# A two-layer decoder trunk on one core: late key splits, gate rows 8 to 15 first, paired gate chunks, products that rotate over eight PSUM banks

## The chip, the cores and the metric

The kernel runs on one core of a Trainium2 chip (trn2). The metric is the device time of one execution in microseconds (us); for the kernel before there are three runs, 1920.1, 1920.73 and 1922.91 us, with the median 1920.73 us. One further execution was taken with the hardware profiler; every row quoted below comes from it.

## What is computed

512 tokens of width 2048 go through two layers. Layer 0 mixes by sparse attention (an indexer chooses 128 keys for each query), layer 1 by stick-breaking attention over one shared K and V. Each layer ends in a LayerNorm over the residual and a sigmoid-gated embedding:

```python
for i in range(DEPTH):                      # two layers
    if i < N_A_LAYERS:
        h = mixer_a(x, w_in_a[i], w_o_a[i], positions)
    else:
        if i == N_A_LAYERS:
            k_sh, v_sh = shared_kv(x, w_kv_b)
        h = mixer_b(x, w_in_b[j], w_o_b[j], k_sh, v_sh)   # sigmoid(z) * prod(1 - sigmoid(z)), o * silu(gate)
    x = layer_norm(ALPHA * x + h, ln_g[i], ln_b[i])
    x = x + (p[i] @ w_p) * sigmoid(x @ w_ple_gate[i])
```

Inputs, weights and the output are f32.

## The kernel before, in words

**Layout.** Activations lie transposed: 16 blocks of 128 features by 512 tokens. Each matrix operand is split into a high part and a low part (`split`, line 129: ScalarE copies the high part, VectorE subtracts it from the source), and each product is three matmuls (`mm3`, line 133): high by high, low by high, high by low. `XH[k]` and `XL[k]` are the two parts of block k of the moving operand; `F` holds 16 f32 blocks. Because all splits go through `split`, most ScalarE and VectorE rows of the profile carry line 111, the recording helper; the tile names tell them apart.

**Weights.** Sync's queue loads them in the order of the list `units` (line 161) into three `raw` buffers of 512 KB (`next_raw`, line 178). A transfer is issued when its buffer is free, and behind every transfer listed earlier. `plain_items` splits each row block into `wh` and `wl`, three buffers of each, so the split of one block waits until TensorE is through with the block three before it. `gemm_w` (line 262) walks 16 row blocks; for each, four banks of PSUM take three matmuls of 512 columns each: 12 matmuls for a block.

**Order.** TensorE's order is written out by hand: generators yield after each three matmuls, and `steps`, `interleave` and `pumped` mix them. The other engines' orders come from a scheduler, except for operations recorded while `pinned` is set (`paced`, and what is popped from the queue `bg` by `pumped`); those keep the written order.

**The phases that the change touches**, in order of time:

- *Start* (lines 138 to 148, 554 to 561). A tile `ones` is made, 24 matmuls of 128 columns run on it, then the indexer's first chunk begins while x and its weights still arrive. Rope tables (`rope_tables`, tiles `ang` and `kk`) are computed on VectorE in between.
- *End of a layer* (`finish_layer`, line 747, once for each layer). Output projection, LayerNorm sums by matmuls with `ones`, embedding, and then the gate's chunks. In lines 914 to 922 `normalise(k+1)` (two VectorE operations on a block, two ScalarE operations with the affine, one VectorE subtraction) is recorded ahead of the four steps that use block k, all 16 blocks in the first 512 columns of the gate. The other chunks (512, 512, 256, 256, or 128 twice in layer 1) follow, with `gated` emptying the banks of the chunk before. Weights come in the list's order, chunk after chunk.
- *K, V and the queries* (lines 995 to 1028). K's projection uses banks 4 to 7. V and four query chunks are computed by a Strassen scheme: `gemm_s` (line 344) accumulates seven products `m0` to `m6` for each chunk, in banks 0 to 6 each time (`product_banks`, line 341). `combine` (line 367) empties them: ScalarE copies m0, m3 and m4, VectorE adds m1, m2, m5 and m6 onto those copies. `turn_values` transposes V through bank 7 while the second chunk runs.
- *Ahead of the attention* (lines 1022 to 1062). The Strassen scheme had overwritten columns 256 to 511 of blocks 0 to 7 with sums, so two transfers from `x2` in DRAM bring them back, and eight `split`s put them in place while the last query chunk runs. Then K of all four groups, V and the first queries are split: K of group 0 by `split`, K of groups 1 to 3 by VectorE copies and GpSimd subtractions. `neg` and `tri` (the constant triangles) are made here.
- *Attention of layer 1* (`sticks`, line 1074, four groups). For each of ten units `logits` makes z by three matmuls, and ScalarE's Abs, Exp, Ln, VectorE's max-and-add, on diagonal units GpSimd's triangle, and a `split` make the parts (`sh`, `sl`) that `weights` multiplies onto z; then Exp, a split (`ah`, `al`), and `values`. It is interleaved with a gate chunk of `w_in_b` (line 1143): 20 steps of it (5 row blocks) ahead of group 0, 8 steps ahead of each other group. At a group's end four Silus empty banks 0 to 3.

Of the kernel before, what the change touches and what calls it, by code (L numbers as in the profile page):

```python
# [18 lines left out]
T = 512  # L19
H = T // 2  # L20
# [57 lines left out]
def trunk_kernel(  # L78
# [63 lines left out]
    ones = top.tile([128, 128], F32R, name="ones")  # L142
    onef = top.tile([128, 128], F32, name="onef")
    dve.memset(onef, 1.0)
    dve.tensor_copy(ones, onef)
    spun = bank(7, "spun")
    for _ in range(24):
        pe.matmul(spun[:, :128], ones, ones, start=True, stop=True)
# [5 lines left out]
    def fblock(n):  # L154
        return F[n // 4][:, n % 4]

# [184 lines left out]
    def product_banks():  # L341
        return [bank(i, f"m{i}").rearrange("p (j t) -> p j t", j=2) for i in range(7)]
# [109 lines left out]
    def add_parts(src, parts):  # L452
        for i, n in enumerate(parts):
            add_job(src, sum(parts[:i]), n)

    def add_finish(layer, w_o):
        add_parts(w_o, PARTS)
        add_job(pT[layer], 0, nk=2)
        for c in range(4):
            add_job(w_ple[layer], c * 512, nk=2)  # L460
        add_parts(w_ple_gate[layer], LAST_PARTS if layer else PARTS)
# [92 lines left out]
    bg.append(lambda: None)  # L554
# [192 lines left out]
    def finish_layer(layer, resid, last, keep, early, ahead):  # L747
# [3 lines left out]
        E8 = keep.enter_context(tc.tile_pool(name=f"e8{layer}", bufs=1, side="right")).tile([128, 8, T], F32, name="E8")  # L751
        fp_ = ExitStack()
        fp = fp_.enter_context(tc.tile_pool(name=f"fp{layer}", bufs=1, side="right"))
        E = [E8[:, n] for n in range(8)] + [fp.tile([128, T], F32, name=f"e{n}") for n in range(8, NK)]
# [11 lines left out]
        def total(parts, b, between):  # L766

            h, l = parts
            ps = bank(b, "sum")
            pe.matmul(ps, ones, h, start=True, stop=False)  # L770
            steps(between, 1)
            pe.matmul(ps, ones, l, start=False, stop=True)
            return ps
# [58 lines left out]
        for c, where in ((1, (0, 1, 2, 3)), (2, (4, 5, 6, 7))):  # L832
            banks, gemm = gemm_part(wo, c, 512, where, 3)
            if c == 1:
                steps(gemm, 36)
                ps = total(parts_of(S), 7, gemm)
                act.activation(cen, ps, AF.Copy, scale=1.0 / 512.0)
# [49 lines left out]
        dve.scalar_tensor_tensor(dm, yps, 1.0 / D, cen, ALU.mult, ALU.subtract)  # L887
        dve.tensor_tensor(va, dm, dm, ALU.mult)
        dve.scalar_tensor_tensor(va, qps, 1.0 / D, va, ALU.mult, ALU.subtract)
# [38 lines left out]
        with tc.tile_pool(name=f"pe{layer}", bufs=1, side="right") as ep:  # L928
# [17 lines left out]
            plan = list(zip(parts[1:], ((2, 3, 4, 5), (6, 7, 0, 1), (2, 3), (0, 1)))) + [(0, ())]  # L946
            if layer:
                plan[3:] = [(128, (0,)), (128, (1,)), (0, ())]
            for c, (n, where) in enumerate(plan):
# [12 lines left out]
                banks = [bank(b, "g") for b in where]  # L962
                gemm = pumped(gemm_w(gitems, plain, banks, n), 4 if n == 512 else 2)
# [13 lines left out]
    def first_sums(E8):  # L977
        shared.append(E8)
        C3.extend(c3_tiles(ps_.enter_context(tc.tile_pool(name="sp0", bufs=1)), range(4)))
        flat = E8.rearrange("p n t -> p (n t)")  # L980
        TF.extend(flat[:, n : n + 3 * H].rearrange("p (i t) -> p i t", i=3) for n in (0, 2 * T))
        T1.extend(flat[:, 4 * T + n * H : 4 * T + (n + 1) * H] for n in range(8))
# [8 lines left out]
    pk_ = ExitStack()  # L991
    finish_layer(0, xT, x2, pk_, first_sums, first_blocks)


    with ps_:
        sp = ps_.enter_context(tc.tile_pool(name="sp1", bufs=1))
        C3.extend(c3_tiles(sp, range(4, 8)))
        Kf, Vf = shared[0][:, 0:4], shared[0][:, 4:8]
        banks = [bank(b, "k") for b in (4, 5, 6, 7)]
# [5 lines left out]
        def turn_values(t):  # L1005
            s = slice(t * 128, (t + 1) * 128)
            ps = bank(7, "vt")
# [4 lines left out]
        for n, dst in enumerate((Vf, *F)):  # L1012
            M = product_banks()
# [18 lines left out]
    tri = pc.tile([128, 128], F32R, name="tri")  # L1032
    neg = pc.tile([128, 128], F32R, name="neg")
    trf = pc.tile([128, 128], F32, name="trf")
    pool.memset(trf, -1.0)
    dve.tensor_copy(neg, trf)
    pool.affine_select(out=trf, in_=trf, pattern=[[-1, 128]], compare_op=ALU.is_ge, fill=0.0, base=0, channel_multiplier=1)
    dve.tensor_copy(tri, trf)

    K = [tuple(pc.tile([128, T], F32R, name=f"k{s}{g}") for s in "hl") for g in range(4)]  # L1040
    V = [tuple(pc.tile([128, 4, 128], F32R, name=f"v{s}{t}") for s in "hl") for t in range(4)]
    items = plain_stream(*[(512, NK, False)] * 4)
    split(*K[0], Kf[:, 0])
    for t in range(4):
        split(*V[t], Vf[:, :, t * 128 : (t + 1) * 128])
    def split_dve(hi, lo, src, eng=dve):
        dve.tensor_copy(hi, src)
        eng.tensor_tensor(lo, src, hi.bitcast(F32), ALU.subtract)

    def split_scaled(g):  # L1050
        Q = []
        for i in range(4):
            qh, ql = (pc.tile([128, 4, 128], F32R, name=f"q{s}", tag=f"q{s}", bufs=4) for s in "hl")
            src = F[g][:, :, i * 128 : (i + 1) * 128]
            act.activation(qh, src, AF.Copy, scale=HSCALE)
            dve.scalar_tensor_tensor(ql, src, HSCALE, qh.bitcast(F32), ALU.mult, ALU.subtract)
            Q.append(tuple(a.rearrange("p h q -> p (h q)") for a in (qh, ql)))
        return Q

    Q = split_scaled(0)  # L1060
    for g in range(1, 4):
        split_dve(*K[g], Kf[:, g], pool)
    pk_.close()
    px_ = ExitStack()
    px = px_.enter_context(tc.tile_pool(name="px", bufs=1, side="right"))
# [74 lines left out]
    for g in range(4):  # L1140
        tc.keep_in_program_order(act.preload_act_table_set("natural_log_exp_and_others"))
        banks = mm_banks("g")
        interleave(sticks(g, Q), 30 + 4, gemm_w(items, plain, banks), 52 - 12 * (g == 0), lead=8 + 12 * (g == 0))
        if g < 3:
            Q = split_scaled(g + 1)
# [4 lines left out]
    px_.close()  # L1150
    pc_.close()

    with ExitStack() as keep:
        finish_layer(1, x2, outT, keep, lambda E8: [], lambda gemm: None)
# [46 lines left out]
```

## Time and profile before

| | us |
|---|---|
| median of three runs | 1920.73 |
| the profiled execution, device time | 1921.26 |
| its span (first to last instruction) | 1919.2 |
| TensorE busy | 1903.6 |
| VectorE busy | 1225.6 |
| ScalarE busy | 929.6 |
| GpSimd busy | 34.2 |

2.06 us of the execution lie outside the span. The mean granted TensorE clock is 0.999. Engines in the rows: PE is TensorE, PEld its weight load, DVE VectorE, ACT ScalarE, POOL GpSimd, SP Sync, whose rows with a q are the issues of transfers. A row of the timeline has the start, the duration, engine, line, operation, tiles written and read, shape and count, and in brackets the idle time of the engine before it and what ended that. A row of the windows has, for each stretch, its length, then busy time and number of instructions of PE, PEld, DVE, ACT and POOL, the granted clock, the share of the DMA engines and GB/s. Successive matmuls overlap, so the distance of their starts, and not the duration of one, tells the rate.

### The profile page before, as it was taken

What the parts mean: (1) busy time and instruction counts of PE and PEld (TensorE: products, weight loads), DVE (VectorE), ACT (ScalarE), POOL (GpSimd) and SP (SyncE); (2) the same over time, 40 slices, a digit from 0 to 9 for tenths busy, and PEclk for the clock granted to TensorE, in tenths of its full rate; (3) what the DMA queues carried; (4) which work ended last, traced back from release to release, by engine and by line L of the source; (5) the groups of instructions that cost most, each with busy time, mean ns of one, the idle gap of its engine ahead of it and who ended that gap; (6) DMA issues with size and microseconds to landing.
All of it is one profiled execution on the core that took longest, in us unless ns stands there. A gap on an engine that the chain in (4) does not pass through costs nothing.

```text
span 1919.2 us, 25113 instructions
## 1 busy us (share of the span) xinstructions
PE 1903.6 (99%) x9247; PEld 1594.0 (83%) x9247; DVE 1225.6 (64%) x2385; ACT 929.6 (48%) x1689; POOL 34.2 (2%) x52
## 2 busy tenths in 40 slices
PE   9999999999999999999999999999999999999998
PEld 7788888888888888878888999987888888887887
DVE  6677667985566445576368788876656645568434
ACT  4355222355555433375235444458877743347323
POOL 0000000000000000000000000011100000000000
PEclk9999999999999999999999999999999999999999
DMA  6332333322222342333334333331222153242333
GB/s 195 99 88 67 99 99 99 95 71 66 66 66 67 125 139 88 99 110 121 115 111 126 104 96 100 108 112 47 70 71 63 59 177 98 77 127 93 120 100 110
DMA packets 110587, 189.22 MB, mean 99 GB/s; under 512 B 8240, under 2 KB 28208, under 8 KB 110464
## 3 DMA queue, kind: packets, MB, share of 16 engines
q1 hardware_dynamic: 110320, 187.33, 32.0%
q8 instruction: 72, 1.18, 0.3%
q14 instruction: 51, 0.42, 0.1%
q0 software_dynamic: 144, 0.30, 0.1%
HBM read 179.21 MB, written 8.39 MB: 98 GB/s over the span
## 4 chain that ended last, share of the span: by engine, by line
PE 93%; DVE 3%; DMA 1%; ACT 1%; issue 1%; POOL 0%; SPq 0%; DVEq 0%
PE g L135 12%; PE g L134 12%; PE g L136 12%; PE o L135 7%; PE o L134 7%; PE o L136 7%; PE m L134 3%; PE m L135 3%; PE m L136 3%; PE q L136 3%; PE q L135 3%; PE q L134 3%; PE z L1114 1%; PE k L134 1%; PE k L136 1%; PE k L135 1%
## 5 line engine op out<-in xcount | busy, mean ns | idle before, releaser
L111 ACT ACTIVATE wh<-raw 128x512 fp32r<-128x512 f32 (+2 forms) x684 | 396.4, 581 | 684.7 <-PE g L135 242.6
L111 DVE TENSOR_TENSOR wl<-raw,wh 128x512 fp32r<-128x512 f32 (+2 forms) x684 | 430.2, 630 | 463.6 <-ACT wh L111 448.0
L134 PE MATMUL g<-xh,wh 128*128 128x512 f32 x1024 | 404.9, 395 | 0.3 <-ACT u L111 0.3
L135 PE MATMUL g<-xl,wh 128*128 128x512 f32 x1024 | 402.0, 393 | 2.0 <-DVE xl L111 2.0
L136 PE MATMUL g<-xh,wl 128*128 128x512 f32 x1024 | 400.7, 391 | 1.3 <-DVE wl L111 1.3
L135 PEld LDWEIGHTS g<-xl,wh 128*128 128x128 f32 x1024 | 192.7, 188 | 44.8 <-DVE xl L111 6.9
L136 PEld LDWEIGHTS g<-xh,wl 128*128 128x128 f32 x1024 | 192.5, 188 | 42.2 <-DVE wl L111 1.8
L134 PEld LDWEIGHTS g<-xh,wh 128*128 128x128 f32 x1024 | 192.9, 188 | 41.4 <-ACT sg L111 1.4
L135 PE MATMUL o<-xl,wh 128*128 128x512 f32 x512 | 199.2, 389 | 0.0
L136 PE MATMUL o<-xh,wl 128*128 128x512 f32 x512 | 199.2, 389 | 0.0
L134 PE MATMUL o<-xh,wh 128*128 128x512 f32 x512 | 199.2, 389 | 0.0
L134 PEld LDWEIGHTS o<-xh,wh 128*128 128x128 f32 x512 | 96.1, 188 | 20.1
L136 PEld LDWEIGHTS o<-xh,wl 128*128 128x128 f32 x512 | 96.1, 188 | 20.0
L135 PEld LDWEIGHTS o<-xl,wh 128*128 128x128 f32 x512 | 96.1, 188 | 19.9
L134 PE MATMUL q<-xh,wh 128*128 128x512 f32 x256 | 99.6, 389 | 0.0
L135 PE MATMUL q<-xl,wh 128*128 128x512 f32 x256 | 99.6, 389 | 0.0
L136 PE MATMUL q<-xh,wl 128*128 128x512 f32 x256 | 99.6, 389 | 0.0
L111 ACT ACTIVATE sh<-st 128x512 fp32r<-128x512 f32 x80 | 50.0, 630 | 82.3 <-PE m L135 44.6
L111 DVE TENSOR_TENSOR sl<-st,sh 128x512 fp32r<-128x512 f32 x80 | 54.8, 690 | 38.4 <-ACT sh L111 38.3
L111 ACT ACTIVATE wk<-z 128x512 f32<-128x512 f32 x80 | 47.4, 592 | 25.7 <-PE z L136 18.6
L134 PEld LDWEIGHTS q<-xh,wh 128*128 128x128 f32 x256 | 48.0, 188 | 10.1
L135 PEld LDWEIGHTS q<-xl,wh 128*128 128x128 f32 x256 | 48.0, 188 | 10.1
(292 smaller groups left out, 3414.2 us busy)
## 6 DMA issues: line engine op xcount, KB each, us to landing
raw<-w_in_a SPq DMA_DIRECT2D x95, 512.0 KB, 3.7
raw<-w_in_b SPq DMA_DIRECT2D x64, 512.0 KB, 3.8
raw<-w_ple_gate SPq DMA_DIRECT2D x52, 512.0 KB, 3.7
raw<-w_o_a SPq DMA_DIRECT2D x24, 512.0 KB, 3.8
raw<-w_o_b SPq DMA_DIRECT2D x24, 512.0 KB, 3.8
raw<-w_kv_b SPq DMA_DIRECT2D x16, 512.0 KB, 3.8
raw<-w_ple_gate SPq DMA_DIRECT2D x24, 256.0 KB, 2.9
f<-xT SPq DMA_DIRECT2D x4, 1024.0 KB, 6.3
```

Of the source, the lines that this page charges most:

```text
L111: ins = method(*args, **kw)
L134: pe.matmul(out, a[0], b[0], start=start, stop=False)
L135: pe.matmul(out, a[0], b[1], start=False, stop=False)
L136: pe.matmul(out, a[1], b[0], start=False, stop=stop)
L1114: pe.matmul(z, m, p, start=False, stop=n == len(terms), skip_group_check=True)
```

## The change

1. **Start.** `ones` is gone. A 128x512 tile of zeros is written and cast into `XL[15]`, and six matmuls of 512 columns run on it. `neg` and `tri` are made at the start as one entry of `bg` (`signs`), and the sums of LayerNorm use `neg` (all -1), with the sign turned in the scale.
2. **End of each layer.** Two chunks of the gate begin together: `gemm_two` takes row blocks two at a time, first for chunk 0 and then for chunk 1, up to block 7; then chunk 0 finishes its blocks 8 to 15, then chunk 1. `normalise` has five steps for a block in place of four. The list of weights follows that order. The later chunks change banks.
3. **K, V and queries.** K uses banks 0 to 3; the products of chunk n begin at bank 4 - n and go round eight banks; V is turned through bank 2.
4. **Returned halves.** The last query chunk has no restoring splits. In the list, the first transfer from `x2` stands behind three weight transfers (row blocks 8 to 13) of the gate's first chunk, the second one behind the fourth (blocks 14 and 15). That chunk now takes row blocks 8 to 15 first, then 0 to 7, and the eight splits are entries of `bg`.
5. **Keys.** K of a group is split (ScalarE and VectorE) as a `bg` entry at the start of the group before it; K has two buffers. The splits of V and of the first queries alternate as `bg` entries of the 20 steps. GpSimd has no splits any more. `E8`, which holds K and V in turn, becomes two tiles, and the work tiles of the attention move to the other side of SBUF.

TensorE's order of operations by kind is the same before and after, but for the six matmuls in place of 24.

```diff
-    ones = top.tile([128, 128], F32R, name="ones")
...
-    for _ in range(24):
-        pe.matmul(spun[:, :128], ones, ones, start=True, stop=True)
+    dve.memset(fblock(0), 0.0)
+    dve.tensor_copy(XL[15], fblock(0))
+    spun = bank(7, "spun")
+    for _ in range(6):
+        pe.matmul(spun, XL[15][:, :128], XL[15], start=True, stop=True)
...
+    PAIRED = [(c, k) for k in range(4) for c in (0, 1)] + [(c, k) for c in (0, 1) for k in range(4, 8)]
+    def gemm_two(items, get, two):
+        for c, k2 in PAIRED:
+            for kb in (2 * k2, 2 * k2 + 1):
+                wh, wl = next(items)
+                for j, out in enumerate(two[c]):
+                    a, b = j * 128, (j + 1) * 128
+                    mm3(out, (wh[:, a:b], wl[:, a:b]), get(kb), kb == 0, kb == NK - 1)
+                    yield
...
-    def product_banks():
-        return [bank(i, f"m{i}").rearrange("p (j t) -> p j t", j=2) for i in range(7)]
+    def product_banks(first):
+        return [bank((first + i) % 8, f"m{i}").rearrange("p (j t) -> p j t", j=2) for i in range(7)]
...
-    units.extend((x2.rearrange("(k p) t -> p k t", p=128)[:, k : k + 4, H:T],) for k in (0, 4))
-    for g in range(4):
+    for k in (4, 5, 6, None, 7, None, 0, 1, 2, 3):
+        if k is None:
+            first = 4 * (units[-1][1] == 14)
+            units.append((x2.rearrange("(k p) t -> p k t", p=128)[:, first : first + 4, H:T],))
+        else:
+            units.append((w_in_b, 2 * k, 2 * k + 1, D, 512))
+    for g in range(1, 4):
         add_job(w_in_b, D + g * 512)
...
+    def signs():
+        trf = ip.tile([128, 128], F32, name="trf")
+        pool.memset(trf, -1.0)
+        dve.tensor_copy(neg, trf)
+        pool.affine_select(out=trf, in_=trf, pattern=[[-1, 128]], compare_op=ALU.is_ge, fill=0.0, base=0, channel_multiplier=1)
+        dve.tensor_copy(tri, trf)
+    bg.append(signs)
...
-        banks = [bank(b, "g0") for b in (6, 7, 0, 1)]
-        gemm = gemm_w(gitems, plain, banks)
-        for k in range(NK):
-            if k < NK - 1:
-                paced(normalise, k + 1)
-            steps(gemm, 4)
-        run(gemm)
+        two = [[bank(b, f"g{c}") for b in where] for c, where in enumerate(((6, 7, 0, 1), (2, 3, 4, 5)))]
+        gemm = gemm_two(gitems, plain, two)
+        for k in range(1, NK):
+            paced(normalise, k)
+            steps(gemm, 5 if k > 1 else 4)
+        steps(gemm, 22)
...
-            M = product_banks()
+            M = product_banks(4 - n)
...
-            if n == 4:
-                for k in range(8):
-                    if k % 4 == 0:
-                        raw = next_raw()
-                    split(XH[k][:, H:T], XL[k][:, H:T], raw[:, k % 4])
...
-    split(*K[0], Kf[:, 0])
-    for t in range(4):
-        split(*V[t], Vf[:, :, t * 128 : (t + 1) * 128])
...
-    for g in range(1, 4):
-        split_dve(*K[g], Kf[:, g], pool)
+    def split_keys(g):
+        K[g] = tuple(pc.tile([128, T], F32R, name=f"k{s}", tag=f"k{s}", bufs=2) for s in "hl")
+        split(*K[g], Kf[:, g])
+    def restore(raw, k):
+        split(XH[k][:, H:T], XL[k][:, H:T], raw[:, k % 4])
+    def gate_items():
+        for k, n in ((0, 6), (4, 2)):
+            yield from plain_items([(512, n, False)])
+            raw = next_raw()
+            bg.extend(lambda raw=raw, k=k: restore(raw, k) for k in range(k, k + 4))
+        yield from plain_items([(512, 8, False), *[(512, NK, False)] * 3])
+    bg.append(lambda: split_keys(0))
+    for i in range(4):
+        bg.append(lambda i=i: split_scaled(0, i))
+        bg.append(lambda i=i: split_values(i))
+    banks = mm_banks("g")
+    gemm = pumped(gate_first(banks))
+    steps(gemm, 20)
...
     for g in range(4):
-        banks = mm_banks("g")
-        interleave(sticks(g, Q), 30 + 4, gemm_w(items, plain, banks), 52 - 12 * (g == 0), lead=8 + 12 * (g == 0))
+        if g:
+            banks = mm_banks("g")
+            gemm = pumped(gemm_w(items, plain, banks))
+        if g < 3:
+            bg.append(lambda g=g: split_keys(g + 1))
+        interleave(sticks(g, Q), 30 + 4, gemm, 52 if g else 40, lead=8 * (g > 0))
```

More of the change, by code (lines that the diff above doesn't have):

```diff
@@ L945, in finish_layer @@
             first = 0
[L946 removed]
+            banks = two[0]
+            plan = list(zip(parts[1:], ((2, 3, 4, 5), (6, 7, 0, 1), (4, 5), (6, 7)))) + [(0, ())]
             if layer:
@@ L961, in finish_layer @@
                     break
-                banks = [bank(b, "g") for b in where]
-                gemm = pumped(gemm_w(gitems, plain, banks, n), 4 if n == 512 else 2)
+                if c:
+                    banks = [bank(b, "g") for b in where]
+                    gemm = gemm_w(gitems, plain, banks, n)
+                else:
+                    banks = two[1]
+                gemm = pumped(gemm, 4 if n == 512 else 2)
                 if c == 3:
@@ L1031, in trunk_kernel @@
     pc = pc_.enter_context(tc.tile_pool(name="pc", bufs=1))
[L1032 to L1040, printed above, removed]
+    K, Q = {}, {}
@@ new lines, in gate_items, with gate_first @@
+    def gate_items():
[4 more added lines that the diff above has]
+        yield from plain_items([(512, 8, False), *[(512, NK, False)] * 3])
+    items = Ahead(gate_items(), 2)
+    def gate_first(banks):
+        for kb in (*range(8, NK), *range(8)):
+            wh, wl = next(items)
+            for j, out in enumerate(banks):
+                s = slice(j * 128, (j + 1) * 128)
+                mm3(out, (wh[:, s], wl[:, s]), plain(kb), kb == 8, kb == 7)
+                yield
```

79 lines of the change are left out of this document (38 added, 41 removed).

## The prediction

> **What bounds the kernel now.** I began with the page: busy times, then the chain that ended last.
>
> ```profile
> span 1919.2 us, 25113 instructions
> PE 1903.6 (99%) x9247; PEld 1594.0 (83%) x9247; DVE 1225.6 (64%) x2385; ACT 929.6 (48%) x1689; POOL 34.2 (2%) x52
> PE 93%; DVE 3%; DMA 1%; ACT 1%; issue 1%; POOL 0%; SPq 0%; DVEq 0%
> ```
>
> TensorE is the bound almost everywhere, and the change leaves its work as it is. So the only thing to win is time in which it waits or starts its matmuls late, and the sum is small against 1919. Busy time hides that, so I compared the number of matmuls in stretches of equal length (windows): LayerNorm's end in both layers, each against a quiet stretch of its own layer, then a change of Strassen products against one ahead of it.
>
> ```profile
> 847.00:882.00 35.00, 34.29 (x147) 26.61 (x146) 30.82 (x50) 25.81 (x36) 0.00 (x0) 1.00 0.28 91
> 900.00:935.00 35.00, 35.00 (x156) 28.97 (x155) 11.24 (x18) 8.83 (x16) 0.00 (x0) 1.00 0.36 111
> 1742.40:1777.40 35.00, 34.28 (x146) 26.60 (x146) 30.78 (x49) 25.79 (x36) 0.00 (x0) 1.00 0.30 91
> 1570.00:1605.00 35.00, 35.00 (x156) 29.01 (x155) 15.66 (x24) 11.29 (x18) 0.00 (x0) 1.00 0.45 144
> 1102.00:1108.00 6.00, 5.49 (x41) 4.87 (x40) 6.00 (x14) 2.48 (x6) 0.00 (x0) 1.00 0.29 89
> 1093.00:1099.00 6.00, 6.00 (x53) 6.00 (x52) 3.95 (x8) 2.30 (x5) 0.00 (x0) 1.00 0.45 133
> ```
>
> At full rate a matmul of 512 columns takes 35.00 / 156 = 0.224 us, one of 256 columns 6.00 / 53 = 0.113. LayerNorm's stretches lack 9 and 10 matmuls, 2.0 and 2.2 us; VectorE is busy for 30.8 of 35 there. The change of products lacks 12, 1.36 us.
>
> **Part by part.** The sum is made against the profiled execution (1921.26, its span 1919.2 and 2.06 outside) and then taken off the median of the runs, 1920.73, which is 0.53 lower.
>
> *Start.* The path to the first wait is made of transfers and VectorE, not of TensorE:
>
> ```profile
> 28.30 0.48 DVE L111 TENSOR_SCALAR ang<-posf,rc 128x512 f32<-128x512 f32 x1
> 30.81 1.29 DVE L111 TENSOR_TENSOR xl<-raw,xh 128x512 fp32r<-128x512 f32 x2 [2.02 <-ACT xh L111]
> 39.51 0.50 PE L136 MATMUL iq<-xh,wl 128*128 128x512 f32 x1 [0.50 <-DVE wl L111]
> ```
>
> The six wide matmuls end earlier than the 24 did, but at 39.51 TensorE waits for `wl` anyhow, so an earlier start is given back there: 0. In the order of the built program `tri` and `ang` now stand between the two subtractions at 30.81, where `ang` had stood in idle time at 28.30. They hold the second one back by 0.4 to 0.5 us, and with it the free buffer, the next transfer of x and the wait at 39.51: +0.5 (bounds 0, if the later `ang` operations fill idle time, and +1.3, with the 0.50 waited there once more and a restart).
>
> *LayerNorm, paired chunks.* Blocks are asked for in pairs at every fourth block time until block 7: 24 matmuls for each pair of `normalise`, and chunk 0 alone uses blocks 8 to 15, which are then long ready. A block costs VectorE three operations and 1.25 to 1.5 `wl`, at 0.6 us apart 2.7 us at most, against five steps, 15 x 0.224 = 3.4 us of TensorE. So VectorE runs ahead, and the waits behind the first go. The first, at block 1, stays (it comes before the second chunk has a step). I take -2.1 for each layer, -4.2 (bounds 0 and -2.7 each, the first wait's 0.6 included). The banks of chunk 0 are emptied in 32 steps in place of 64: six entries, one each four steps, 8 places; covered by 96 matmuls (21 us), and without that cover some 0.6 us an entry.
>
> *Strassen.* Who frees the banks at such a change:
>
> ```profile
> 1100.63 0.58 ACT L111 ACTIVATE u<-m 128x512 f32<-128x512 f32 x1
> 1101.60 1.09 ACT L111 ACTIVATE E<-m 128x512 f32<-128x512 f32 x2 [0.39 <-PE m L136]
> 1102.09 0.68 DVE L111 TENSOR_TENSOR E<-m,u 128x512 f32<-128x512 f32 x1
> 1103.02 0.68 DVE L111 TENSOR_TENSOR u<-m,u 128x512 f32<-128x512 f32 x1
> 1104.56 0.68 DVE L111 TENSOR_TENSOR E<-m,E 128x512 f32<-128x512 f32 x1
> 1102.48 0.28 PE L134 MATMUL m<-xh,wh 128*128 128x256 f32 x1
> 1103.76 0.38 PE L134 MATMUL m<-c3h,sh 128*128 128x256 f32 x1 [0.31 <-DVE u L111]
> 1105.30 0.39 PE L134 MATMUL m<-xh,sh 128*128 128x256 f32 x1 [0.20 <-DVE E L111]
> PE m L134 <- DVE u L111: 1.2, 4, 0.3
> ```
>
> The new chunk starts at 1102.48, and a product takes three matmuls, 0.36 us. Old m0 is free at 1101.21, m1 at 1102.77, m2 at 1103.70, m3 and m4 by 1102.69, m5 at 1105.24. Going round one bank on, new m0 finds an empty bank, m1 to m6 take old m0 to m5. m2 is wanted at 1103.20 (free), m3 at 1103.56 (waits 0.2 for old m2), m4 and m5 are free, m6 is wanted at 1104.94 (waits 0.36 for old m5). With 0.1 for each restart, about 0.75 is left of 1.36: -0.6, four times, -2.4 (bounds 0 and -1.36 each). VectorE's order there is unchanged. The change from the last query chunk to the gate finds the same banks as before: 0. K in banks 0 to 3 and V turned in bank 2 meet the same order of emptying: 0, covered by the eight steps between the last turn and the next chunk (24 x 0.12 = 2.9 us).
>
> *Ahead of and in group 0.* The dearest place:
>
> ```profile
> 1271.19 0.50 PE L134 MATMUL g<-xh,wh 128*128 128x512 f32 x1 [0.28 <-ACT u L111]
> 1285.08 0.39 PE L134 MATMUL z<-qh,kh 128*128 128x512 f32 x1
> 1286.47 0.50 PE L135 MATMUL z<-ql,kh 128*128 128x512 f32 x1 [1.00 <-DVE ql L111]
> 1289.02 0.79 PE L136 MATMUL g<-xh,wl 128*128 128x512 f32 x1 [1.35 <-DVE wl L111]
> 1290.03 0.63 PE L135 MATMUL z<-ql,kh 128*128 128x512 f32 x1
> 1290.46 0.63 PE L136 MATMUL z<-qh,kl 128*128 128x512 f32 x1
> 1295.72 0.40 PE L1114 MATMUL z<-sh,tri 128*128 128x512 f32 x1
> 1300.77 0.50 PE L135 MATMUL o<-al,vh 128*128 128x512 f32 x1 [0.31 <-DVE al L111]
> 1278.03 2.18 ACT L111 ACTIVATE vh<-E 128x512 fp32r<-128x512 f32 x4
> 1266.09 1.03 ACT L111 ACTIVATE xh<-raw 128x256 fp32r<-128x256 f32 x3 [2.13 <-DMA raw<-x]
> 1282.31 1.28 ACT L111 ACT_TABLE_LOAD   x1
> 1291.50 0.64 POOL L1072 TENSOR_SCALAR_AFFINE_SELECT wk<-wk 128x512 f32<-128x512 f32 x1 [8.03 <-DVE wk L111]
> raw<-w_in_b SPq DMA_DIRECT2D x64, 512.0 KB, 3.8
> DMA to landing us min/median/max: 3.6/4.3/5.0
> ```
>
> The 60 matmuls from 1271.19 to 1285.08 stay. Before, VectorE was late behind three K copies and four V and four query subtractions, so TensorE stood for 1.00 and 1.35 us; then it ran at half rate (starts 0.43 apart at 1290.03 and 1290.46), some 1.6 us more. Afterwards VectorE has K of group 0 alone, and the four queries between the V parts: from 1277.3, at 0.6 apart, nine operations end by 1282.7, well ahead of 1285.08. Both waits go. The eight restoring splits leave the last query chunk, where TensorE had no wait from them (0), and come here.
>
> What is late next: ScalarE, in order. Block 14's `wh` needs block 11 done (four blocks of 2.78 behind 1271.19, 1282.3). Then at 0.54 a copy (2.18 / 4) and 0.34 a half (1.03 / 3): that copy, four halves, the table load of 1.28, block 15's `wh`, K of group 1, and unit 0's Abs starts at 1286.6; Abs, a query copy, Exp and Ln end at 1288.75; VectorE's 0.7 and the triangle's 0.64 give 1290.2. But behind Ln on ScalarE stand Abs of unit 1 (to 1289.3), block 0's `wh` (its transfer goes out when the halves are subtracted, about 1285.9, plus 3.8: to 1290.3), three more halves (to 1291.3; their transfer, out at 1283.9, landed within 5.0), Exp (to 1291.9), and only then unit 0's `sh` (1292.5) and VectorE's `sl` (1293.2). TensorE is there after 27 matmuls, 1285.08 + 6.1 = 1291.2: it waits 1.3 and 0.5. The same reckoning gives 0.45 for unit 1's `sl`, and `al` of unit 0 at 1297.9 in place of 1300.77: -2.9. Bounds: from 1285.08 to 1300.77 TensorE starts 44 matmuls, 10.0 us at 0.227, so no more than 5.7 can go; and if the added 3.3 us of ScalarE (eight halves, K of group 1) show in full, 0 is won.
>
> Does 1.8 us of waiting bring the half rate back? 2.35 within 2.9 us did (rows above), 1.36 within 3.3 us at a change of products did not (clock 1.00 in its window). 1.8 is nearer to 1.36, by little: I leave it out of the sum. The Trainium skill, in "TensorE: Matmul & The Clock Gate", section "What's actually happening", lets the half rate follow at least one idle window of about 3.4 us; by that rule it would not come back here, and the sum would be the same, but the rule would not have let it come at 1289 either, so the trace does not bear it out.
>
> *Keys of groups 2 and 3.* One ScalarE copy now stands ahead of the last Silu of groups 0 and 1.
>
> ```profile
> 1344.18 0.61 ACT L111 ACTIVATE wk<-g 128x512 f32<-128x512 f32 x1
> 1345.10 0.39 PE L134 MATMUL g<-xh,wh 128*128 128x512 f32 x1
> ```
>
> That Silu ends at 1344.79 and TensorE wants the bank at 1345.10; 0.54 later makes a wait of 0.25 and a restart, +0.3, twice, +0.6 (bounds 0 and +1.1). Sums with `neg`, the two tiles for `E8` and GpSimd's lighter load: 0, the operations and places being the same or off the path.
>
> **Sum:** +0.5 - 4.2 - 2.4 - 2.9 + 0.6 = -8.4, that is 1912.3.
>
> **Rivals.** (B) One half-rate stretch at the new wait: six to eight matmuls 0.2 late, 1.6, less the 0.9 of later waits that it swallows: 1913.0. For: 1.8 lies between the two rows. (C) ScalarE pays for the added 3.3 us and nothing is won in group 0: 1915.2. For: its queue is full behind that place:
>
> ```profile
> 1300.00:1320.00 20.00, 19.64 (x84) 15.40 (x84) 13.84 (x22) 17.98 (x34) 2.30 (x3) 1.00 0.17 53
> ```
>
> (D) Pairing doesn't do what it says: `wl` waits in VectorE's queue for TensorE to free a buffer, and the `xl` behind it stays late: 1916.5, at the edge of no change. Against: each such `xl` stands five steps or more ahead of its use. (E) The waits that I leave go too, since each depends on some tenths: first block 0.9 for both layers, products 1.6, unit 0's `sh` 1.3: 1908.5. (F) Slower: the half rate stays through group 0 (1285 to 1343), because ScalarE, with 17.98 of 20 us busy, makes TensorE stand again in each stretch of 3.4 us. Each costs 1.7; from the fifth on all is lost, and eight give 1925.9. For: the trace shows the first of them. Against: after one, TensorE was back at 84 matmuls in 20 us, and a slower TensorE lets ScalarE catch up.
>
> **How the numbers follow.** Chances: forecast 0.53, B 0.15, C 0.08, D 0.09, E 0.09, F 0.06. Measurement can tell about 0.2% (3.8 us) from no change, so faster means below 1916.9: forecast, B, C and E, 0.85; within: D, 0.09; slower: F, 0.06. The range runs from 1907.5 (E and a little) to 1917.0 (D), leaving out F and the ends at which all bounds fall together.
>
> **What would show it.** LayerNorm's stretches with 155 or 156 matmuls in 35 us and one wait for `xl` a layer, not five; the waits of `m` for `u` gone, shorter ones one product later; no wait for `ql` or `wl` at 1285 to 1289 and a new one for `sh` and `sl` of unit 0, at full clock; the first long wait at 40.0 rather than 39.5. I am wrong if ScalarE's halves keep TensorE standing beyond 1294, if the clock stays low there, or if the paired blocks still wait.

## The result, and the profile after

The changed kernel takes 1912.5 us (median of five runs, 1911.99 to 1913.52) against 1920.85 (five runs, 1920.1 to 1922.91): 0.9955 of the time before, 95% interval 0.9941 to 0.997. The forecast was 1912.3. Its profiled execution took 1912.5 us, 1.8 of them outside the span.

From the page after come the span, the busy times and the shares of the chain that ended last; then, from the windows, LayerNorm's end in both layers and a change of Strassen products, at the places that were shown of before:

```profile
span 1910.7 us, 25058 instructions
PE 1896.1 (99%) x9229; PEld 1589.2 (83%) x9229; DVE 1225.0 (64%) x2385; ACT 931.1 (49%) x1692; POOL 28.9 (2%) x49
PE 93%; DVE 3%; ACT 2%; DMA 1%; issue 1%; SPq 0%; DVEq 0%; ACTq 0%
```

```profile
847.00:882.00 35.00, 35.00 (x157) 28.95 (x156) 28.15 (x44) 22.68 (x33) 0.00 (x0) 1.00 0.33 104
1735.70:1770.70 35.00, 35.00 (x156) 28.98 (x155) 27.89 (x43) 22.57 (x33) 0.00 (x0) 1.00 0.32 100
1099.50:1105.50 6.00, 5.76 (x46) 5.35 (x45) 6.00 (x14) 2.39 (x5) 0.00 (x0) 1.00 0.32 89
```

LayerNorm's stretches hold 157 and 156 matmuls in place of 147 and 146, with VectorE at 28 of 35 us; the change of products holds 46 in place of 41. Of the waits that TensorE still has, these lie at the start, in LayerNorm and in the attention, where the change was meant to act (in total, times, longest):

```profile
PE iq L136 <- DVE wl L111: 1.9, 3, 0.9
PE z L1159 <- ACT sh L111: 1.6, 2, 1.1
PE z L1159 <- DVE sl L111: 0.7, 3, 0.3
PE g L135 <- DVE xl L111: 0.6, 2, 0.3
```

One wait for `xl` a layer is left. The waits of `g` for `wl`, of `z` for `ql` and of `m` and `g` for `u` are gone from the list, and `sh` and `sl` of the attention are new. Each measurement below has its own runs of before, with medians from 1920.68 to 1921.02; so a difference of a few tenths between two measurements says nothing.

Both kernels issue the same matmuls in the same order (the first few dozen, which only spin, aside), so the start of the n-th can be set beside the start of the n-th. This table, made from the two traces, is the ledger against which the forecast's terms are held:

| place | before | after | gained so far |
|---|---|---|---|
| last long wait of the first projection | 73.14 | 73.08 | 0.06 |
| ahead of LayerNorm, layer 0 | 816.38 | 816.51 | -0.13 |
| behind it | 936.82 | 934.80 | 2.02 |
| last query chunk, behind four changes | 1252.88 | 1248.50 | 4.38 |
| gate, ahead of group 0 | 1284.86 | 1279.78 | 5.08 |
| group 0, behind the values of unit 0 | 1301.34 | 1293.28 | 8.06 |
| group 0, behind unit 3 | 1312.09 | 1304.97 | 7.12 |
| group 2, begun | 1418.28 | 1411.96 | 6.32 |
| ahead of LayerNorm, layer 1 | 1724.46 | 1718.18 | 6.28 |
| last matmul | 1913.99 | 1905.49 | 8.50 |

### The profile page after: what moved, and what is told of

Its sections match the earlier page's. It is cut to its first block, busy times and chain, and to the rows that moved or that the text cites. A ratio compares the mean times of both kernels' runs of the same rounds, so it can differ in the third digit from the quotient of the medians.

```text
span 1910.7 us, 25058 instructions
## 1 busy us (share of the span) xinstructions
PE 1896.1 (99%) x9229; PEld 1589.2 (83%) x9229; DVE 1225.0 (64%) x2385; ACT 931.1 (49%) x1692; POOL 28.9 (2%) x49
## 4 chain that ended last, share of the span: by engine, by line
PE 93%; DVE 3%; ACT 2%; DMA 1%; issue 1%; SPq 0%; DVEq 0%; ACTq 0%
PE g L134 12%; PE g L135 12%; PE g L136 12%; PE o L136 7%; PE o L135 7%; PE o L134 7%; PE m L134 3%; PE m L135 3%; PE m L136 3%; PE q L134 3%; PE q L135 3%; PE q L136 3%; PE z L1159 2%; PE k L136 1%; PE k L135 1%; PE k L134 1%
## 5 line engine op out<-in xcount | busy, mean ns | idle before, releaser
L111 DVE TENSOR_TENSOR xl<-f,xh 128x512 fp32r<-128x512 f32 x80 | 54.3, 686 | 11.4 <-ACT f L111 11.0
L136 PEld LDWEIGHTS q<-xh,wl 128*128 128x128 f32 x256 | 48.1, 188 | 10.0
```

The costliest lines, as they stand in the source:

```text
L111: ins = method(*args, **kw)
L136: pe.matmul(out, a[1], b[0], start=False, stop=stop)
```

## The experiments

"Before" in each measurement stands for runs on the same chip as the kernel that is timed.

**1. pair_alone.** The kernel before with `gemm_two`, its order of weights and the five steps:

```diff
...
+        gemm = gemm_two(gitems, plain, two)
+        for k in range(1, NK):
+            paced(normalise, k)
+            steps(gemm, 5 if k > 1 else 4)
...
```

> The kernel before with the two gate chunks of LayerNorm's end begun together, and nothing else of the change. My theory: VectorE was late because a block's three operations and its weights had only four steps of TensorE to lie beside; with five, all waits for xl but the first of each layer go, a stretch of 35 us behind the first block holds 155 or 156 matmuls in place of 147 and 146, and the time falls by 2.1 us a layer, 4.2 in all, to 1916.6. Rival: the gain seen there came with the other edits (the sums with the negative tile, the two E tiles, where things lie); then the waits for xl stay here and the time stays above 1919.

1916.42 us (10 runs) against 1921.02: ratio 0.9977 (0.9968 to 0.9986). The windows of this kernel, with xcount behind the busy time:

```profile
847.00:882.00 35.00, 35.00 (x156) 29.00 (x155) 28.12 (x43) 22.57 (x32) 0.00 (x0) 1.00 0.32 102
1740.00:1775.00 35.00, 35.00 (x156) 28.97 (x155) 27.71 (x43) 22.51 (x33) 0.00 (x0) 1.00 0.32 98
```

The pairing alone fills both stretches, and one wait for `xl` a layer is left in its list; the rival falls. Reckoned as in the ledger, each layer gains 2.19 us.

**2. turn_alone.** The kernel before with the banks' rotation only:

```diff
...
-        banks = [bank(b, "k") for b in (4, 5, 6, 7)]
+        banks = [bank(b, "k") for b in range(4)]
...
-            M = product_banks()
+            M = product_banks(4 - n)
...
```

> The kernel before with the Strassen chunks going round the eight banks (and the banks of the last gate parts, of K and of the turned V that go with it). My theory: each of the four changes of products loses 0.7 to 0.76 us in place of 1.24 to 1.36, with waits of about 0.2 and 0.36 us one product later; -2.4 us, 1918.4. The wait for u of 0.28 us ahead of the gate's first matmul stays, since I now put it down to the restoring copies that stand ahead of u on ScalarE. Rival: the new banks took that wait too; then the gate's first matmul starts without one and the time is 1917.7.

1917.78 us (11 runs) against 1921.02: ratio 0.9983 (0.9974 to 0.9992). In its trace the four changes win 2.39 us, as forecast. The wait ahead of the gate is still there:

```profile
1269.05 0.50 PE L134 MATMUL g<-xh,wh 128*128 128x512 f32 x1 [0.28 <-ACT u L111]
```

So the rival's reason falls, although its time was met: in the profiled execution (1917.18 us) another 1.6 us went because the half rate in group 0 is missing there. Experiment 11 takes that up.

**3. turn_back.** The same with `product_banks(4 + n)`, and V turned in bank 4.

> As turn_alone, but round the banks the other way: a new product takes the bank of the old product one behind it, and the last takes the empty one. My theory counts by when each old bank comes free: new m0 waits 0.3 us for old m1, m1 0.5 for m2, m4 0.35 for m5, m5 0.15 for m6, with the restarts some 1.6 us a change against 1.35 before: no gain, 1920.9 to 1921.9. Rival: a spare bank alone is what helps, whichever way one goes round; then it gains what turn_alone gains, 1918.4.

1922.3 us (11 runs) against 1921.02: ratio 1.0007 (0.9998 to 1.0016), 0.4 above what I had given. The VectorE operation that frees old m1, and the three waits at a change:

```profile
1103.17 0.68 DVE L111 TENSOR_TENSOR E<-m,u 128x512 f32<-128x512 f32 x1
...
1103.91 0.39 PE L134 MATMUL m<-xh,wh 128*128 128x256 f32 x1 [0.19 <-DVE E L111]
...
1104.85 0.39 PE L134 MATMUL m<-xh,wh 128*128 128x256 f32 x1 [0.31 <-DVE u L111]
...
1106.38 0.39 PE L134 MATMUL m<-xh,sh 128*128 128x256 f32 x1 [0.20 <-DVE E L111]
```

The first product now waits for old m1, which is empty at 1103.17 + 0.68 = 1103.85. A spare bank in itself gives nothing: which old bank a product inherits decides. By the ledger's reckoning the four changes cost 1.4 us more than before. The time alone doesn't show this: in the profiled execution the half rate in group 0 is missing, which takes 1.6 off, and the matmul of 73.14 starts 1.1 later.

**4. halves_after.** The kernel before with its eight halves returned behind the last chunk's combinations:

```diff
...
-            if n == 4:
-                for k in range(8):
...
         drain()
+        for k in range(8):
+            if k % 4 == 0:
+                raw = next_raw()
+            paced(split, XH[k][:, H:T], XL[k][:, H:T], raw[:, k % 4])
```

> The kernel before with its eight halves returned after the last Strassen chunk's combinations instead of in it. My theory for the 0.7 us that the change gained at the gate's first matmul, where I had forecast nothing: u of the last products stood on ScalarE behind a half that waited until TensorE had used the old half for the last time. Then the wait of 0.28 for u at 1271.19 is gone here, though nothing else of the change is in. The halves then stand ahead of the keys on ScalarE and VectorE, so the waits for wl and ql grow by about 2.8: 1923. Rival: the wait for u hangs on the banks or on VectorE and is seen here as well.

1925.79 us (9 runs) against 1920.68: ratio 1.0024 (1.0014 to 1.0034). I had the price too low: this gate begins with block 0, whose halves it needs, so TensorE waits up to 4.1 us for `xl`, and one stretch of 6.83 us, two of 3.41, runs at half rate. The wait for `u` is gone, and `u` comes earlier against the last product:

```profile
1270.55 0.58 ACT L111 ACTIVATE u<-m 128x512 f32<-128x512 f32 x1
...
1271.51 0.28 PE L136 MATMUL m<-c3h,wl 128*128 128x256 f32 x1
```

`u` ends at 1271.13, before the last product's last matmul starts. But the same gate matmul now waits for a half of block 0, so this is support for the cause, not a clean isolation of it. The traces of before (first two rows) and after (last two) say the same more directly:

```profile
1270.24 0.42 ACT L111 ACTIVATE xh<-raw 128x256 fp32r<-128x256 f32 x1 [1.29 <-PE m L136]
1270.56 0.58 ACT L111 ACTIVATE u<-m 128x512 f32<-128x512 f32 x1
```

```profile
1264.48 0.58 ACT L111 ACTIVATE u<-m 128x512 f32<-128x512 f32 x1
1266.38 0.40 PE L134 MATMUL g<-xh,wh 128*128 128x512 f32 x1
```

Before, `u` stood behind a half that waited 1.29 us until TensorE was through with the old one. After, nothing stands there, and the gate starts without a wait.

**5. signs_first.** The changed kernel with `neg` and `tri` made ahead of everything, from a scratch part of `F[0]`:

```diff
...
-    bg.append(signs)
+    bg.append(lambda: None)
...
```

> The changed kernel with the two sign tiles made at the very start, so that neither they nor ang stand between the two subtractions of x at 31 us. Theory A: what TensorE or VectorE gains in the first 40 us is given back at the waits behind, at the latest at the one of 0.47 us at 73 us, which hangs on a transfer: the wait of 0.87 at 32.80 shrinks to about 0.3, later ones grow, the matmul at 73.1 starts within 0.2 us of where it did, and the time is 1912.5. Theory B (the step of my forecast): the sign tiles hold the chain back; then that matmul starts 0.5 us earlier, and the time is 1912.0.

1910.55 us (five runs, 1909.55 to 1910.87), 1.95 less than the changed kernel; no run of the one reaches a run of the other. VectorE in the changed kernel, then in this one:

```profile
30.59 0.22 DVE L111 CAST tri<-trf 128x128 fp32r<-128x128 f32 x1
30.73 0.48 DVE L111 TENSOR_SCALAR ang<-posf,rc 128x512 f32<-128x512 f32 x1
31.12 0.69 DVE L111 TENSOR_TENSOR xl<-raw,xh 128x512 fp32r<-128x512 f32 x1
```

```profile
30.60 0.69 DVE L111 TENSOR_TENSOR xl<-raw,xh 128x512 fp32r<-128x512 f32 x1
```

The second subtraction is 0.52 us earlier (0.32 of that already at the first of the pair), the one of the next pair 1.1, and the matmul of 73.08 starts at 71.58, 1.5 earlier. Theory A falls. B has the right sign and a quarter to a third of the size: I had counted one pair of subtractions, but in the changed kernel an `ang` operation stands between the next pair too (36.02 to 37.23; here they run back to back).

**6. spins_narrow.** The changed kernel with the matmuls ahead of the first projection as before:

```diff
-    for _ in range(6):
-        pe.matmul(spun, XL[15][:, :128], XL[15], start=True, stop=True)
+    for _ in range(24):
+        pe.matmul(spun[:, :128], XL[15][:, :128], XL[15][:, :128], start=True, stop=True)
```

> The changed kernel with 24 matmuls of 128 columns at the start in place of the six of 512, as before, so that the first projection starts 1.6 us later. Theory A (the step of my forecast: an earlier start is given back at the wait for wl at 39 us): the matmul at 73.1 starts where it did, 1912.5. Theory B (the start counts, and the sign tiles took back what it had gained): that matmul starts 1.0 to 1.6 us later, 1913.5 to 1914.1.

1912.64 us (five runs, 1911.65 to 1913.04): no difference from the changed kernel. In the trace the projection starts 2.2 us later, the matmul of 73.08 starts 1.4 later (as B has it), and 0.6 of that comes back in group 0. One execution does not settle it, though: in six traces whose first operations are the same (before, before_again, pair_alone, turn_alone, turn_back, halves_after) that matmul starts at 73.14, 73.14, 73.43, 73.37, 74.22 and 73.96, and in the five of the changed start (the changed kernel, table_first, halves_late, halves_twice, keys_late) anywhere from 73.08 to 73.76. Here it starts at 74.45, outside these five, but with the narrow matmuls the scheduler also put other splits first on ScalarE and VectorE. What the six wide matmuls are worth stays open, between nothing and 1.4. The gain of signs_first is clear of this spread: its 71.58, and 70.80 with the same edit in experiment 12, lie ahead of all five.

**7. table_first.** The changed kernel with ScalarE's table load for group 0 ahead of the first gate chunk:

```diff
+    tc.keep_in_program_order(act.preload_act_table_set("natural_log_exp_and_others"))
     bg.append(lambda: split_keys(0))
```

> The changed kernel with the table load of group 0 (1.28 us on ScalarE, at 1279.14 there) put ahead of the first gate chunk, at 1266, where ScalarE has time. My theory: what ends the wait for sh of unit 0 at 1287.41 is ScalarE's order, in which block 0's wh stands ahead of it and waits until 1284.76 for a transfer that went out at 1280.36; a lighter queue ahead of that transfer changes little: the wait of 1.12 stays within 0.3, 1912.2. Rival (C of the forecast: the sum of ScalarE's work counts): the wait falls by the whole 1.28 and is gone, 1911.0.

1912.56 us (five runs): no difference in the time. 1.28 us of ScalarE's work left the queue, and the wait for `sh` went from 1.12 to 0.8. By the starts, the stretch that takes the changed kernel from 1279.78 to 1290.07 is 0.35 us shorter here, and this execution was 0.68 later at the first projection, which hides it in the profiled time. The rival falls: of the 1.28 taken out only 0.35 shows, so it isn't the sum of ScalarE's work.

**8. halves_late.** The changed kernel with the second four halves behind block 1's weights:

```diff
-    for k in (4, 5, 6, None, 7, None, 0, 1, 2, 3):
+    for k in (4, 5, 6, None, 7, 0, 1, None, 2, 3):
...
-        for k, n in ((0, 6), (4, 2)):
+        for k, n in ((0, 6), (4, 6)):
...
```

> The changed kernel with the second four returned halves loaded after block 1's weights instead of after block 15's, so that block 0's transfer goes out 1.9 us earlier and three copies of halves no longer stand ahead of unit 0's sh on ScalarE. My theory (that order sets the wait): sh of unit 0 is ready when the triangle is, at about 1285.9, so the waits of 1.12 and 0.22 for it shrink to 0.4 at most together, the one at 1301 by half a us or more, since there too sh comes ahead of the next Abs; 1910.0 to 1911.0. Rival (the chain from z through Abs, Exp, Ln, VectorE and GpSimd's triangle is simply that long): the waits stay, 1912.5.

1910.37 us (five runs, 1910.1 to 1911.16), 2.13 less than the changed kernel. Group 0 there, ScalarE and TensorE, ahead of unit 0 and then of unit 3:

```profile
1284.76 0.63 ACT L111 ACTIVATE wh<-raw 128x512 fp32r<-128x512 f32 x1 [0.50 <-DMA raw<-w_in_b]
1285.30 1.01 ACT L111 ACTIVATE xh<-raw 128x256 fp32r<-128x256 f32 x3
1286.22 0.61 ACT L111 ACTIVATE wk<-wk 128x512 f32<-128x512 f32 x1
1286.74 0.61 ACT L111 ACTIVATE sh<-wk 128x512 fp32r<-128x512 f32 x1
1287.41 0.50 PE L1159 MATMUL z<-sh,tri 128*128 128x512 f32 x1 [1.12 <-ACT sh L111]
1288.14 0.50 PE L1159 MATMUL z<-sl,tri 128*128 128x512 f32 x1 [0.22 <-DVE sl L111]
...
1298.82 1.02 POOL L1117 TENSOR_SCALAR_AFFINE_SELECT run<-run 128x512 f32<-128x512 f32 x1 [4.30 <-DVE run L111]
1299.97 0.60 ACT L111 ACTIVATE wk<-z 128x512 f32<-128x512 f32 x1 [1.42 <-PE z L136]
1300.46 0.62 ACT L111 ACTIVATE sh<-run 128x512 fp32r<-128x512 f32 x1
1301.14 0.50 PE L1159 MATMUL z<-sh,tri 128*128 128x512 f32 x1 [0.51 <-ACT sh L111]
```

and in halves_late:

```profile
1285.35 0.63 ACT L111 ACTIVATE sh<-wk 128x512 fp32r<-128x512 f32 x1
1286.17 0.39 PE L1159 MATMUL z<-sh,tri 128*128 128x512 f32 x1
...
1298.10 0.63 ACT L111 ACTIVATE sh<-run 128x512 fp32r<-128x512 f32 x1 [1.33 <-POOL run L1117]
1298.63 0.58 ACT L111 ACTIVATE wk<-z 128x512 f32<-128x512 f32 x1
1299.07 0.40 PE L1159 MATMUL z<-sh,tri 128*128 128x512 f32 x1
```

In the changed kernel `sh` of unit 0 stands behind a weight copy that waits for a transfer, three halves and an Exp; without that wait and the three halves it starts 1.39 us earlier and TensorE doesn't wait for it. At unit 3 the scheduler now puts `sh` ahead of the next Abs. The triangle had been ready at 1299.84 and `sh` began 0.62 later, so by these rows that order made the wait of 0.51 there. The order on ScalarE sets both waits, as theory had it.

**9. halves_twice.** The changed kernel with each half's copy made twice:

```diff
-        split(XH[k][:, H:T], XL[k][:, H:T], raw[:, k % 4])
+        for _ in range(2):
+            act.activation(XH[k][:, H:T], raw[:, k % 4], AF.Copy)
+        dve.tensor_tensor(XL[k][:, H:T], raw[:, k % 4], XH[k][:, H:T].bitcast(F32), ALU.subtract)
```

> The changed kernel with each of the eight returned halves copied twice on ScalarE, some 0.33 us each. My theory (ScalarE's order sets the wait for sh of unit 0): the wait of 1.12 grows to about 3, and with it a 3.41 us window of the clock is idle for more than six tenths, so that one window at half rate follows, 1.4 us more: 1915.8. Without the half rate 1914.3. Rival (the chain through GpSimd is the limit): 1912.5 to 1913.

1915.63 us (7 runs, 1915.07 to 1916.3). The wait for unit 0's `sh` grew to 3.55 us, and one stretch of 3.41 us at half rate followed: theory, in both parts.

**10. keys_late.** The changed kernel with the next group's keys split behind the four Silus:

```diff
-        if g < 3:
-            bg.append(lambda g=g: split_keys(g + 1))
         interleave(sticks(g, Q), 30 + 4, gemm, 52 if g else 40, lead=8 * (g > 0))
...
+        if g < 3:
+            paced(split_keys, g + 1)
```

> The changed kernel with the keys of the next group split after the group's four Silu instead of ahead of the last of them. My theory: the two waits for a bank of g at 1338 and 1404 (0.29 and 0.24 beyond the usual distance, 0.4 each with what follows) go, -0.8; group 0 also loses one ScalarE copy ahead of unit 0, but its sh now stands behind another Ln: within 0.4 of before; 1911.7. Rival: the keys are then late at the start of the next group, whose first z waits for kl: 1912.5 or more.

1911.62 us (five runs, 1911.21 to 1912.79), 0.88 less than the changed kernel, though the two sets of runs overlap. At group 0's end the changed kernel has the key copy ahead of the last Silu, which ends at 1338.20:

```profile
1337.07 0.64 ACT L111 ACTIVATE kh<-E 128x512 fp32r<-128x512 f32 x1
1337.59 0.61 ACT L111 ACTIVATE wk<-g 128x512 f32<-128x512 f32 x1
1338.25 0.50 PE L134 MATMUL g<-xh,wh 128*128 128x512 f32 x1
```

With the copy behind it the two changes of group win 0.4 each by the starts, and no `z` waits for the keys.

**11. before_again, and the half rate.** The kernel before once more.

> The kernel before once more, for a second look at the half rate. If it follows from the two waits of 1.00 and 1.35 us alone, it is seen again at 1289. If it follows from the idle share of one window of a fixed grid of 3.41 us, whose place against the program differs from one execution to the next, then it depends on where the grid falls: none if the two waits are divided between two windows so that neither is idle for more than six tenths (then 1.4 us less), one if they fall into the same.

The half rate was seen again at 1289 (1921.24 us). In before the clock was full for 1280.00 us up to the half rate, half for 3.413 and full again for 624.64, that is 375, 1 and 183 times 3.413; the other traces divide the same way. So the clock changes on a grid of 3.413 us, and each trace's grid can be laid from its own changes. For each trace, windows of the grid in order of time; the columns are as in the windows of before, PE's busy time first and the clock third from the end. First pair_alone, then turn_alone, which has the same two waits of 1.0 and 1.34 us, then halves_twice:

```profile
1284.31:1287.72 3.41, 1.80 (x7) 1.19 (x8) 3.41 (x8) 2.27 (x4) 0.00 (x0) 1.00 0.00 0
1287.72:1291.13 3.41, 3.41 (x10) 2.67 (x9) 1.75 (x3) 1.23 (x2) 0.64 (x1) 0.50 0.80 231
```

```profile
1284.15:1287.57 3.42, 1.90 (x7) 1.29 (x8) 3.42 (x8) 2.27 (x4) 0.00 (x0) 1.00 0.00 0
1287.57:1290.98 3.41, 3.41 (x17) 2.82 (x16) 2.06 (x4) 2.31 (x5) 0.64 (x1) 1.00 0.75 249
```

```profile
1285.25:1288.66 3.41, 1.65 (x8) 1.03 (x6) 2.00 (x4) 2.60 (x8) 0.16 (x1) 1.00 0.44 164
1288.66:1292.08 3.42, 1.40 (x5) 0.96 (x6) 2.10 (x5) 2.94 (x8) 0.54 (x1) 1.00 0.00 0
1292.08:1295.49 3.41, 3.41 (x10) 2.63 (x9) 1.90 (x3) 2.92 (x7) 1.22 (x2) 0.50 0.00 0
```

The half rate came in the window behind one in which TensorE was busy for 1.23 (before), 1.35 (before_again), 1.80 (pair_alone) or 1.40 us (halves_twice). It did not come behind 1.90 (turn_alone) or 2.07 us (the changed kernel), nor in turn_back, where the same two waits fall into two windows with 2.23 us each. So where the grid falls decides, with the same waits. But behind 1.65 us it came in halves_after and did not come in halves_twice (the first row there): busy time as the profile gives it doesn't mark the border, and what exactly counts in a window stays open.

**12. three_parts.** The changed kernel with the edits of signs_first, halves_late and, for groups 2 and 3, keys_late.

> The changed kernel with three of the edits together: the sign tiles made at the start, the second four halves returned four blocks later, and the keys of groups 2 and 3 split behind the last Silu (those of group 1 stay where the change put them). If the three gains belong to different places, as I read the traces, they add: 1912.5 less 1.95, 2.1 and 0.8 is 1907.6, with no wait for sh of units 0 and 3 and none for a bank of g at 1335 and 1401. Rival: the earlier ones only move a wait to a later place (the returned halves now meet the fuller part of ScalarE's queue); then 1908.5 to 1910.

1907.14 us (five runs, 1907.06 to 1908.01), 0.993 of before (0.9916 to 0.9943) and 5.36 less than the changed kernel; the single gains make 1.95 + 2.13 + 0.88 = 4.96. They add, within 0.4; some of the surplus lies at the start, where the matmul of 73.08 starts at 70.80, another 0.8 ahead of signs_first. Of `sh` no wait is left in its list, and of `sl` little; it is the fastest kernel of this study.

```profile
PE z L1158 <- DVE sl L111: 0.5, 2, 0.3
```

## Why the prediction was right, and which of its parts were not

The total was met to 0.2 us, the signs of all large terms too. By the ledger:

| term | forecast | measured |
|---|---|---|
| start | +0.5 | +0.1 (816.38 to 816.51) |
| LayerNorm, both layers | -2.1 and -2.1 | -2.15 and -2.22 |
| four changes of products | -2.4 | -2.36 |
| gate's first matmul | 0 | -0.70 |
| group 0 | -2.9 | -2.04 |
| keys of groups 2 and 3 | +0.6 | +0.80 |
| rest of the span | 0 | +0.04 |
| sum | -8.4 | -8.50 in the span, -0.26 outside it |

- **LayerNorm: right in mechanism and size.** One wait a layer stays; the pairing alone does it (experiment 1).
- **Products: right, down to the single wait.** Forecast 0.2 for old m2 and 0.36 for old m5, and 0.1 more for each restart (the matmul behind a wait starts later than its usual distance). Against the usual 0.12 the two waiting matmuls start 0.20 and 0.35 us late (the second behind one at 1102.81), and the next ones, at 1101.98 and 1103.51, another 0.1 each: 0.75 in all. turn_back, reckoned from the same times of emptying, came out as it should.

```profile
1101.43 0.28 PE L136 MATMUL m<-c3h,sl 128*128 128x256 f32 x1
1101.75 0.39 PE L134 MATMUL m<-c3h,sh 128*128 128x256 f32 x1
...
1103.29 0.39 PE L134 MATMUL m<-c3h,wh 128*128 128x256 f32 x1 [0.20 <-DVE E L111]
```

- **Gate's first matmul: a step failed.** "The eight restoring splits leave the last query chunk, where TensorE had no wait from them (0)": it had. The row that I quoted, the wait of 0.28 for `u` at 1271.19, was theirs, through ScalarE's order. -0.7 in place of 0.
- **Group 0: right to the values of unit 0, too good behind.** Forecast -2.9 to there, measured 8.06 - 5.08 = 2.98: ahead of unit 0's `sh`, with both waits and the half rate of before gone, the gain so far had been 9.60, and 1.54 of it is given back up to there. The waits for `sh` and `sl` were put at 1.3 and 0.5, and by the distances of the starts TensorE lost 1.28 and 0.50. (The terms that the forecast prints for this stretch, 10.0 of matmuls and 1.3, 0.5 and 0.45 of waits, reach 1297.3 and not 1297.9; restarts of 0.1 and 0.25 at `al`, which it does not print, stand in the trace.) I then followed only units 0 and 1. Unit 3 waits for `sh` again, and 0.94 is given back. That rival C's ground (a fuller ScalarE) is real and its price not, experiments 7 and 8 show together.
- **GpSimd's lighter load: put at 0 without need.** VectorE was late in the kernel before not only by the number of its operations. While GpSimd made its three key subtractions, these rows of VectorE were long:

```profile
1278.68 4.09 POOL L1048 TENSOR_TENSOR kl<-E,kh 128x512 fp32r<-128x512 f32 x3 [0.93 <-DVE kh L111]
1280.28 1.32 DVE L111 CAST neg<-trf 128x128 fp32r<-128x128 f32 x1
1281.52 1.79 DVE L111 TENSOR_TENSOR kl<-E,kh 128x512 fp32r<-128x512 f32 x1
```

In the changed kernel the same cast takes 0.22 and the same subtraction 0.69; the last of the three K copies took 1.52 beside 0.43 for the first. That makes some 3.3 us, more than the two waits of 1.00 and 1.35 together. An estimate from these rows is that the waits would have gone with GpSimd's splits alone; no run takes them out alone, nor the new order of the splits alone, so which of the two was needed stays open.
- **Half rate: the right outcome by a wrong measure.** I compared sums of waits, 1.8 with 2.35 and 1.36. But with the same two waits it came in three executions and not in two others, by where the grid fell (experiment 11). Whether it stayed away in the changed kernel by luck, and how near rival B was, the runs don't show; with the wait grown to 3.55 us it came (experiment 9).
- **Start: a step failed, and something unknown covered it.** The sign tiles' place costs about 1.95 us (experiment 5), not 0.5. As the projection is not later at 73 us than before, something won that back; that the profiled execution began well is not enough, since the four others with the same start lie at 73.28 to 73.76, still within the range of before. The earlier start is the one candidate that I know (the forecast put it at 0), but experiment 6 doesn't show it in the time. This stays open.
- **Keys: right, 0.4 each in place of 0.3.**

Measured less forecast, the terms were off by -0.4, -0.7, +0.9 and +0.2 (start, gate, group 0, keys); these happened to cancel, and the total was better than its parts.

## What to carry to other kernels

Where the bound engine is 99% busy, compare counts of instructions in equal stretches, and reckon each wait from the time at which the buffer it inherits comes free: that was good to 0.1 us here, in both directions of rotation. On an engine that serves several streams in order, the sum of its work says little; look for what stands ahead of the late operation and itself waits (a transfer, a last use), and follow every unit of the stage, not the first two. An edit that is free by its own duration can cost several times that where it stands between two operations that free transfer buffers. And before counting operations on an engine, compare the duration of each with the same one elsewhere in the trace: three rows of VectorE had grown by 1.1 us each, and a count didn't see it.

## What the runs showed of the hardware

- TensorE's granted clock changed here only on a grid of 3.413 us, at another place in each execution (the half rate began at 1289.05 in before and at 1289.19 in before_again). With the same waits it came in before, before_again and pair_alone and not in turn_alone or turn_back, and it was worth 1.6 us: from the matmul of 1284.86 to the one of 1298.22 the first three took 13.36 or 13.37 us, the other two 11.76. The Trainium skill, in "TensorE: Matmul & The Clock Gate", section "What's actually happening", has the free-running window of 3413 ns, and the traces agree. It names an idle window as the condition; here a window in which TensorE was busy for 1.80 us, over half, was enough. The measurement decides.
- Beside GpSimd's subtractions three operations of VectorE took 1.52, 1.32 and 1.79 us in place of 0.43, 0.22 and 0.69. In halves_after VectorE's rows at that place stayed short (0.43, 0.23 and 0.69), and GpSimd's first subtraction took 7.89 us in place of 1.40. So one or the other was slower when the two overlapped; the traces don't show why, nor what decides which.
- The same first operations brought the matmul of 73.14 us anywhere from 73.14 to 74.22 in six executions: a difference of a microsecond at the start can't be read from one trace.
